# Zero-padded low key parts in the differential attention, and one buffer pool for raw and split weights

## The chip, the core and the metric

The kernel runs on one core of a Trainium2 chip. The metric is the device time of one execution in microseconds (us). Work goes to five engines that run at the same time: TensorE (PE in the profile; its weight loads are shown apart, as PEld), VectorE (DVE), ScalarE (ACT), GpSimd (POOL), and SyncE (SP), which here only issues DMAs.

## What is computed

One inference step of a two-layer diffusion backbone over 640 tokens: 512 latent tokens (a grid) and 128 context tokens. Each layer normalises its input, applies a shift and a scale, sends it through one input projection, runs three branches (latent attention "MLA", a short gated convolution, and differential attention), gates them, and adds the output projection to the residual. The change is in the differential attention, which has 4 heads with two score maps each:

```python
q = q.reshape(b, n, DIFF_HEADS, 2, DIFF_QK)          # DIFF_QK = 64
k_all = jnp.concatenate([k_ctx, rope(k)], axis=1)    # 512 latent + 128 cached keys
s = jnp.einsum('bqhad,bkhad->bhaqk', q, k_all) * scale
p = jax.nn.softmax(s, axis=-1)
a = p[:, :, 0] - lam_full * p[:, :, 1]
o = jnp.einsum('bhqk,bkhe->bqhe', a, v_all)
```

## The kernel before

Channels lie on the 128 partitions and tokens on the free axis; the 640 tokens are worked in two halves of 320 (`HB`). To get float32 accuracy from single-pass products, operands are split into a high part (rounded to `float32r`) and a low part (the rest); `mm3` (L347 to L352) makes three products of each pair: high with high, high with low, low with high.

**Input projection.** The weights come in 15 units per layer of mostly 256 columns, plus 4 units of the output projection. `load_unit` (L301) loads a unit in two halves into raw tiles (L307, L308), rounds them to the high part on ACT (L312), and subtracts on DVE, or on POOL for a few units, for the low part (L314). The raw tiles have a pool of 3 buffers (tag `raw`), the high and low tiles one of 9 (tag `w`, `wtiles`, L286). `unit(n, k=1)` asks for unit n and starts the next. The scratch tile `tb` of `silu_bcast` (L138) is a raw tile too.

**Differential attention, one head.** `q_post` (L537) rotates the queries and writes `qs[:, a, :]` for each of the two maps a: on the 64 partitions of that map the high part of q, on the other 64 its low part (L543, L544). `k_post` (L548) rotates the keys to `kf`, writes `kh[:, a, :]` (the high part of the map's keys on both halves of the partitions, L562 and L564) and the low part `kl` for all 128 channels at once, in one DVE instruction of 128x640 (L559). The tile `kl` is taken from the pool `blk` of 39 general slots (`slot`, `NBLK`).

`diff_unit` (L587) does 128 queries: for each map a and each half j of the keys two products into the same PSUM region, with `qs` as the stationary operand (loaded as weights, on PEld) and the keys as the moving one:

```python
TE.matmul(ps[:, j, 0:HB], qs[:, a, qc], kh[:, a, js], start=True, stop=False)    # L603: 128 rows
TE.matmul(ps[:, j, 0:HB], qs[own, a, qc], kl[own, js], start=False, stop=True)   # L604: 64 rows
```

The first contracts over 128 rows (high and low q with high k), the second over the map's own 64 (high q with low k). There are 2 layers x 4 heads x 4 query tiles x 2 maps x 2 halves = 128 of each. Then DVE takes the row maximum (L613), scales it (L614), ACT takes the exponential (L620), DVE the reciprocal (L622), the factor (L623) and the combination of both maps (L625); a later stage transposes (L582) and multiplies with the values (L634).

**Order.** The queues are filled by a program that interleaves generators: `main` (projections), `bg` (work of other engines: `q_post`, `k_post`, weight loads), `side` (the modulation vectors of this and the next layer: DMAs at L147 and pairs of multiply-and-sum instructions on DVE, L152), and the attention units. Each attention unit moves the projections on by 5 steps of 6 products. The framework then puts each engine's instructions in a fixed order, gives tiles their slots and sets the waits; an allocation waits until a slot of its tag is released. Each engine runs its queue in order.

Of the kernel before, what the change touches and what calls it, by code (L numbers as in the profile page):

```python
# [15 lines left out]
ALU = mybir.AluOpType  # L16
# [12 lines left out]
# the parts of the two halves of the tokens: from, to, stream  # L29
# [9 lines left out]
# The input projection is read in units of 256 columns (dv0, dv1: 272, for the rotary keys are with  # L39
# them; cq1: 128), in the order of use.  # L40
# [20 lines left out]
def tile_kernel(ctx: ExitStack, tc: tile.TileContext, i: dict, o: dict):  # L61
# [11 lines left out]
    NBLK, NW, NRAW = 39, 9, 3  # L73
# [17 lines left out]
    # ---------------------------------------------------------------- constants  # L91
# [19 lines left out]
    # products of zeros warm the tensor engine up while the first loads are under way  # L111
# [7 lines left out]
    # silu of the two conditioning vectors, with channels on partitions  # L119
# [6 lines left out]
    # modulation: mod[l][part] is [P, KT, 2 streams]  # L126
    mod = [[cst.tile([P, KT, 2], F32, name="mod%d_%d" % (l, s)) for s in range(3)] for l in range(DEPTH)]

    # the rest on the vector engine: rows of the transposed weights times the broadcast silu,
    # one half of the channels after the other  # L130
# [3 lines left out]
    def silu_bcast(hf, name):  # L134
        for c in range(2):
            pin(nc.sync.dma_start(out=cb2[:, c, :],
                                  in_=i["cond2"][c:c + 1, hf * 512:(hf + 1) * 512].broadcast_to([P, 512])))
        tb = wp.tile([P, 2, 512], F32, tag="raw", name="tb" + name, bufs=NRAW)  # L138
        S.activation(tb, cb2, AF.Tanh, scale=0.5)
        V.tensor_scalar(out=tb, in0=tb, scalar1=0.5, scalar2=0.5, op0=ALU.mult, op1=ALU.add)  # L140
        V.tensor_tensor(out=cb2, in0=cb2, in1=tb, op=ALU.mult)
# [14 lines left out]
    def ada_fin(l, s, ks=slice(0, KT)):  # L156
        """adds the bias; the scale becomes norm_g * (1 + scale)"""
# [9 lines left out]
    # -lambda of each layer, and subln * (1 - lambda_init) / 2  # L167
# [19 lines left out]
    # ---------------------------------------------------------------- helpers  # L187
    def rsqrt(v, n, name):
        """1/sqrt of a small [p, n] tile of positive numbers: a bit-level start y, then a y' = a y (t^2 + b t / a + c / a),
        t = v y^2, which is right to 2e-5, and a Newton step from there"""  # L190
# [14 lines left out]
    def rstd_half(accs, n, name):  # L205
        """accs, each [P, 320]: squares, to be summed over all of them and over the partitions; gives 1/rms on all
        partitions in PSUM. Three overlapping tiles of 128 tokens cover the half."""
# [15 lines left out]
    class Norm:  # L223
        """collects the squares of one half of the tokens over the k tiles"""
# [32 lines left out]
    bg = []            # work of the other engines that goes along with that of the tensor engine  # L257
# [7 lines left out]
    def split(src, name):  # L265
        """the halves of the tokens of src, each as a high and a low part"""
# [19 lines left out]
    def wtiles(w, name, tag):  # L286
        """room for the high and the low part of half a unit"""
        if tag == "w":
            return [wp.tile([P, 4, w], F32R, tag="w", name="w%s%s" % (c, name), bufs=NW, padded_shape=[P, 4, 272])
                    for c in "hl"]  # L290
        f = kh_tile if tag == "kh" else lambda nm: qs_tile(nm, T)
        return [f("w%s%s" % (c, name)).rearrange("p a n -> p (a n)")[:, 0:4 * w].rearrange("p (k c) -> p k c", k=4)
                for c in "hl"]
# [7 lines left out]
    def load_unit(src, w, name, tags, eng, res):  # L301
        """src [2, P, 4 * w] in DRAM -> tiles of the high and the low parts"""
        raws = []
        for hf in range(2):
            if hf == 1 and len(loaded) == 1:
                yield
            raws.append(wp.tile([P, 4, w], F32, tag="raw", name="r%s%d" % (name, hf), bufs=NRAW, padded_shape=[P, 4, 272]))  # L307
            pin(nc.sync.dma_start(out=raws[hf], in_=src[hf]), len(loaded) < 3)  # L308
        yield
        for hf in range(2):  # L310
            hi, lo = wtiles(w, "%s%d" % (name, hf), tags[hf])
# [16 lines left out]
    def unit(n, k=1, only_load=False, halves=2):  # L328
        """weights of unit n; those of the next k are on their way"""
# [12 lines left out]
    def wtile(n, kt, cs):  # L342
        """high and low parts of the columns cs of k tile kt of unit n"""
# [3 lines left out]
    def mm3(ps, aa, bb, first=True, last=True):  # L347
        """ps (+)= aa.T @ bb for operands split into high and low parts"""
# [5 lines left out]
    late = []          # low parts that are still to be taken  # L354

    def scaled(l, j, kt, rb, xs):
        """x / rms * norm_g * (1 + scale) of half j"""
# [7 lines left out]
    def modulate(l, j, kt, rb, xs, hs, last=False, t=None):  # L365
        """h = x / rms * norm_g * (1 + scale) + shift of half j, k tile kt, as high and low parts; the low part of a
        k tile follows the product of the next one"""
# [28 lines left out]
    # ---------------------------------------------------------------- start  # L396
# [9 lines left out]
    # Shift and scale of the first layer, in blocks of 512 columns: 0 and 1 of the shift, 2 and 3 of the scale. The  # L406
    # tensor engine sums three of them over the k tiles, the vector engine one, for which the tensor engine adds up the
    # partitions.
# [10 lines left out]
    def load_start(*what):  # L419
        """the next k tile of a block, or "x" for the first half of the next tile of x"""  # L420
# [78 lines left out]
    for l in range(DEPTH):  # L499
# [3 lines left out]
        def proj(nm, b, j):  # L503
            """128 columns (block b of unit nm) of half j of the tokens, channels on partitions"""
# [17 lines left out]
        def rope(dst, src, cos, sin, mask, name, rs=slice(0, P), eng=V):  # L522
            """dst = rotated latents of src, on the partitions rs"""
# [12 lines left out]
        # ------------------------------------------------ differential attention, one head  # L536
# [11 lines left out]
        def k_post(h, k, res):  # L548
# [6 lines left out]
            kl = slot("kl" + tg, F32R)  # L555
# [748 lines left out]
```

## Time and profile before

| what | value |
|---|---|
| device time, 3 runs | 873.0, 874.47, 876.0 us (median 874.47) |
| span of the profiled execution, first to last instruction | 871.4 us |
| PE busy | 836.4 us (96%) |
| DVE busy | 629.3 us (72%) |
| ACT busy | 445.4 us (51%) |
| mean granted TensorE clock | 0.983 |

The profile comes from one execution, for which no device time apart from its span is listed; the span is 1.6 us under the shortest of the three runs and 3.1 us under the median. "Busy" of PE counts overlapping products once. In a timeline, the distance from one product's start to the next is what a product costs; its duration is longer, since products overlap. An "idle before" entry names what ended the idle time.

### The profile page before, as it was taken

The numbers are of one execution on the slowest core, as the hardware profiler recorded it, in microseconds if no ns is written. First come the engines' busy times: TensorE is split into PE (matmuls) and PEld (weight loads), VectorE is DVE, ScalarE is ACT, GpSimd is POOL, SyncE is SP. The second block draws the span as 40 slices with busy tenths as digits, with TensorE's granted clock in tenths as the row PEclk, the third lists the DMA queues.
The fourth block names the chain that finished last, engine by engine and source line by source line (L and its number), as shares of the span: only waits on it lengthen the run. The fifth ranks groups of instructions, "written<-read, shape, count | busy, mean of one in ns | idle before, by whom it ended". The sixth has DMA issues, their size and how long they took to land.

```text
span 871.4 us, 14318 instructions
## 1 busy us (share of the span) xinstructions
PE 836.4 (96%) x5390; PEld 755.1 (87%) x5390; DVE 629.3 (72%) x1481; ACT 445.4 (51%) x978; POOL 70.3 (8%) x45
## 2 busy tenths in 40 slices
PE   6999999999999998999999999999999999999995
PEld 1399788888989897999999988888898999999994
DVE  4887887798878778689577778777667656667535
ACT  2265445454647566565345444545464666767210
POOL 3300020030000202000220002003000020200000
PEclk9999999999999999899999999999999999999997
DMA  8916343031401332134831324302030011110503
GB/s 316 364 44 212 104 125 116 24 120 63 147 21 61 94 118 66 39 109 147 280 97 43 124 74 128 121 19 77 4 103 25 26 49 49 49 50 16 179 1 120
DMA packets 66164, 85.52 MB, mean 98 GB/s; under 512 B 4976, under 2 KB 47408, under 8 KB 66096
## 3 DMA queue, kind: packets, MB, share of 16 engines
q1 hardware_dynamic: 65520, 83.96, 30.1%
q8 instruction: 42, 0.69, 0.3%
q10 hardware_dynamic: 576, 0.66, 0.2%
q14 instruction: 26, 0.21, 0.1%
HBM read 78.14 MB, written 6.46 MB: 97 GB/s over the span
## 4 chain that ended last, share of the span: by engine, by line
PE 70%; DVE 12%; ACT 8%; DMA 6%; issue 3%; SPq 1%; DVEq 0%; ACTq 0%
PE S L604 4%; PE wo L351 4%; PE wo L352 4%; PE wo L350 4%; PE S L603 4%; PE O L634 3%; DVE jk L152 2%; PE p1qk L350 2%; PE p1qk L352 2%; PE p1qk L351 2%; PE Om L906 2%; DMA ada<-in_adaA 2%; PE p0c L352 2%; PE tpm L889 2%; PE p1c L350 2%
## 5 line engine op out<-in xcount | busy, mean ns | idle before, releaser
L152 DVE CUSTOM_DVE_ANT_0 jk<-at,cb 128x512 bf16<-128x512 f32 x128 | 92.2, 720 | 2.0 <-DMA at<-in_adaT 1.1
L620 ACT ACTIVATE E<-S,sm 128x640 f32<-128x640 f32 (+1 forms) x80 | 56.0, 708 | 70.3 <-DVE sm L614 51.4
L351 PE MATMUL wo<-mx,who 128*128 128x320 f32 x256 | 79.2, 310 | 0.1
L352 PE MATMUL wo<-mx,wlo 128*128 128x320 f32 x256 | 78.9, 309 | 0.0
L350 PE MATMUL wo<-mx,who 128*128 128x320 f32 x256 | 78.4, 310 | 0.0
L613 DVE TENSOR_REDUCE sm<-S 128x1 f32<-128x640 f32 (+1 forms) x80 | 56.4, 714 | 25.1 <-PE S L604 24.3
L603 PE MATMUL S<-kh,qs 128*128 128x320 f32 x128 | 49.4, 386 | 3.7 <-ACT E L620 3.7
L604 PE MATMUL S<-kl,qs 64*128 64x320 f32 x128 | 52.6, 411 | 0.0
L878 ACT ACTIVATE Em<-Sm,smm 128x640 f32<-128x640 f32 (+1 forms) x40 | 28.4, 709 | 43.9 <-DVE smm L876 41.7
L351 PEld LDWEIGHTS wo<-mx,who 128*128 128x128 f32 x256 | 48.1, 188 | 0.7 <-DVE mx L273 0.4
L352 PEld LDWEIGHTS wo<-mx,wlo 128*128 128x128 f32 x256 | 48.1, 188 | 0.0
L235 ACT ACTIVATE sqn<-xn 128x320 f32<-128x320 f32 x32 | 15.1, 471 | 64.4 <-DVE xn L1152 62.6
L350 PEld LDWEIGHTS wo<-mx,who 128*128 128x128 f32 x256 | 47.8, 188 | 0.0
L352 PE MATMUL v<-whi_dv,hl 128*128 128x272 f32 x160 | 46.2, 289 | 0.0
L350 PE MATMUL v<-whi_dv,hh 128*128 128x272 f32 x160 | 46.1, 288 | 0.0
L351 PE MATMUL v<-wli_dv,hh 128*128 128x272 f32 x160 | 46.0, 288 | 0.0
L634 PE MATMUL O<-v,atd 128*128 128x128 f32 x336 | 43.9, 274 | 0.0
L314 POOL TENSOR_TENSOR wli_c<-ri_c,whi_c 128x1024 fp32r<-128x1024 f32 x8 | 20.5, 2562 | 280.1 <-PE p1zm L351 97.8
L350 PE MATMUL p0c<-hh,whi_c 128*128 128x320 f32 x128 | 42.1, 329 | 0.0
L350 PE MATMUL p0qk<-hh,whi_qk 128*128 128x320 f32 x128 | 40.6, 328 | 1.4 <-ACT hh L378 1.4
L634 PEld LDWEIGHTS O<-v,atd 128*128 128x128 f32 x336 | 41.9, 191 | 0.0
L604 PEld LDWEIGHTS S<-kl,qs 64*128 64x128 f32 x128 | 23.5, 184 | 21.2 <-issue 20.4
(375 smaller groups left out, 2669.9 us busy)
## 6 DMA issues: line engine op xcount, KB each, us to landing
at<-in_adaT SPq DMA_DIRECT2D x64, 256.0 KB, 3.9
ada<-in_adaA SPq DMA_DIRECT2D x32, 256.0 KB, 5.0
ri_qk<-in_wi SPq DMA_DIRECT2D x16, 512.0 KB, 4.1
ri_c<-in_wi SPq DMA_DIRECT2D x16, 512.0 KB, 3.7
ro<-in_wo SPq DMA_DIRECT2D x16, 512.0 KB, 4.1
ri_dv<-in_wi SPq DMA_DIRECT2D x8, 544.0 KB, 4.0
ri_zd<-in_wi SPq DMA_DIRECT2D x8, 512.0 KB, 3.9
x<-in_xT SPq DMA_DIRECT2D x16, 160.0 KB, 4.8
```

The source lines that it names most:

```text
L152: V.tensor_tensor_reduce(out=junk, in0=raw, in1=cb2[:, c, :], scale=1.0, scalar=0.0, op0=ALU.mult, op1=ALU.add, accum_out=acc)
L314: eng.tensor_tensor(out=lo, in0=raws[hf], in1=hi.bitcast(F32), op=ALU.subtract)
L350: TE.matmul(ps, ah, bh, start=first, stop=False)
L351: TE.matmul(ps, ah, bl, start=False, stop=False)
L352: TE.matmul(ps, al, bh, start=False, stop=last)
L603: TE.matmul(ps[:, j, 0:HB], qs[:, a, qc], kh[:, a, js], start=True, stop=False)
L604: TE.matmul(ps[:, j, 0:HB], qs[own, a, qc], kl[own, js], start=False, stop=True)
L613: V.tensor_reduce(out=sm[:, a:a + 1], in_=Sv[a], axis=AX.XY if u < 4 else AX.X, op=ALU.max)
L620: S.activation(ev, Sv[a], AF.Exp, bias=sm[:, 2 + a:3 + a], scale=DIFF_SCALE, accum_out=so)
L634: TE.matmul(po[:, 0:128], at[:, c * 128:(c + 1) * 128], vv[:, h * 128:(h + 1) * 128], start=c == 0, stop=c == n - 1)
L878: S.activation(e if u < 4 else e[:, 0:128], Sv, AF.Exp, bias=sm[:, 1:2], scale=MLA_SCALE, accum_out=sm[:, 2:3])
L889: TE.transpose(tp[:, c * 128:(c + 1) * 128], toktile(e, c), ident)
```

## The change

The low key parts get two permanent tiles, `klz[0]` and `klz[1]` (128x2x640 each), used in turn by the heads. `klz[h % 2][:, a, :]` holds the low part of map a on that map's own 64 partitions and zeros on the other 64; the zeros are written once, by `clear_klz`, in layer 0. The subtraction that makes the low part is done per map, on 64 partitions. The second product then has the same 128-row stationary operand as the first; the zeros cancel the rows of low q. Memory for this comes from the general slots (39 to 37), which hold no `kl` any more, and from the weights: raw and split weight tiles, and `tb`, share one pool of 11 buffers in place of 3 + 9. The rest of the diff removes comments.

```diff
-    NBLK, NW, NRAW = 39, 9, 3
+    NBLK, NW = 37, 11
...
-        tb = wp.tile([P, 2, 512], F32, tag="raw", name="tb" + name, bufs=NRAW)
+        tb = wp.tile([P, 1024], F32, tag="w", name="tb" + name, bufs=NW, padded_shape=[P, 1088])
+        tb = tb.rearrange("p (c n) -> p c n", c=2)
...
+    klz = [cst.tile([P, 2, T], F32R, name="klz%d" % n) for n in range(2)]
+
+    def clear_klz():
+        z = slot("klz0")
+        V.memset(z, 0.0)
+        for t in klz:
+            for a in range(2):
+                oth = slice(64 - a * 64, 128 - a * 64)
+                V.tensor_copy(t[oth, a, :], z[oth])
...
-            raws.append(wp.tile([P, 4, w], F32, tag="raw", name="r%s%d" % (name, hf), bufs=NRAW, padded_shape=[P, 4, 272]))
+            raws.append(wtile_new(w, "r%s%d" % (name, hf), "w", F32))
...
-            hi, lo = wtiles(w, "%s%d" % (name, hf), tags[hf])
+            hi = wtile_new(w, "wh%s%d" % (name, hf), tags[hf], F32R)
+            lo = wtile_new(w, "wl%s%d" % (name, hf), tags[hf], F32R)
...
-            kl = slot("kl" + tg, F32R)
+            kl = klz[h % 2]
             hk = slot("hk" + tg, F32R)
             S.copy(hk, kf)
             yield
-            V.tensor_tensor(out=kl, in0=kf, in1=hk.bitcast(F32), op=ALU.subtract)
             for a in range(2):
                 own, oth = slice(a * 64, a * 64 + 64), slice(64 - a * 64, 128 - a * 64)
+                V.tensor_tensor(out=kl[own, a, :], in0=kf[own], in1=hk[own].bitcast(F32), op=ALU.subtract)
                 S.copy(kh[own, a, :], kf[own, :])
...
-                    own = slice(a * 64, a * 64 + 64)
...
                         TE.matmul(ps[:, j, 0:HB], qs[:, a, qc], kh[:, a, js], start=True, stop=False)
-                        TE.matmul(ps[:, j, 0:HB], qs[own, a, qc], kl[own, js], start=False, stop=True)
+                        TE.matmul(ps[:, j, 0:HB], qs[:, a, qc], kl[:, a, js], start=False, stop=True)
...
             if l == 0:
+                clear_klz()
                 prep_small()
```

`wtile_new(w, name, tag, dt)` gives one tile of the tag that `wtiles` gave two of. `clear_klz` is called after the first five token tiles of the values' first half, before the attention of head 0 begins.

## Rows read from the trace of the kernel before

**Rows 1.** The page, parts 1 and 2: busy time of an engine with its share of the span, and the granted TensorE clock in 40 slices of the span, in tenths (9 is 90% or more).

```profile
PE 836.4 (96%) x5390; PEld 755.1 (87%) x5390; DVE 629.3 (72%) x1481; ACT 445.4 (51%) x978; POOL 70.3 (8%) x45
...
PEclk9999999999999999899999999999999999999997
```

**Rows 2.** The page, part 4: the chain of work that ended last, by engine and by engine and line.

```profile
PE 70%; DVE 12%; ACT 8%; DMA 6%; issue 3%; SPq 1%; DVEq 0%; ACTq 0%
PE S L604 4%; PE wo L351 4%; PE wo L352 4%; PE wo L350 4%; PE S L603 4%; PE O L634 3%; DVE jk L152 2%; PE p1qk L350 2%; PE p1qk L352 2%; PE p1qk L351 2%; PE Om L906 2%; DMA ada<-in_adaA 2%; PE p0c L352 2%; PE tpm L889 2%; PE p1c L350 2%
```

**Rows 3.** Groups of TensorE instructions by line and shape: tile written and tiles read, shapes, count, busy us and mean ns of one, idle before. S is the score tile of the differential attention, Sm that of the MLA.

```profile
L604 PE MATMUL S<-kl,qs 64*128 64x320 f32 x128 | 52.6, 411 | 0.0
L603 PE MATMUL S<-kh,qs 128*128 128x320 f32 x128 | 49.4, 386 | 3.7 <-ACT E L620 3.7
...
L351 PE MATMUL Sm<-kml,qmh 96*128 96x320 f32 x64 | 20.1, 314 | 0.0
```

**Rows 4.** Timeline of TensorE products around the scores of one unit (both maps, eight products) in layer 0: start us, duration us, line, tiles, shapes. The two last lines are projection products.

```profile
213.05 0.31 PE L603 MATMUL S<-kh,qs 128*128 128x320 f32 x1
213.29 0.41 PE L604 MATMUL S<-kl,qs 64*128 64x320 f32 x1
213.62 0.41 PE L603 MATMUL S<-kh,qs 128*128 128x320 f32 x1
...
215.34 0.41 PE L604 MATMUL S<-kl,qs 64*128 64x320 f32 x1
215.67 0.41 PE L350 MATMUL p0qk<-hh,whi_qk 128*128 128x320 f32 x1
215.93 0.31 PE L351 MATMUL p0qk<-hl,whi_qk 128*128 128x320 f32 x1
```

**Rows 5.** Timeline of the weight loads (PEld): two of that unit, with the idle time before them, and one of an MLA unit.

```profile
213.62 0.19 PEld L603 LDWEIGHTS S<-kh,qs 128*128 128x128 f32 x1 [0.15 <-issue]
213.97 0.18 PEld L604 LDWEIGHTS S<-kl,qs 64*128 64x128 f32 x1 [0.16 <-issue]
...
315.45 0.19 PEld L350 LDWEIGHTS Sm<-kmh,qmh 96*128 96x128 f32 x1
```

**Rows 6.** Timeline of TensorE: a score product of 128 rows and the 128-row product after it; then the first and the last of 17 products in a row of 320 columns, five of them scores of the MLA with 96 rows, the others projection products with 128.

```profile
266.13 0.31 PE L603 MATMUL S<-kh,qs 128*128 128x320 f32 x1
266.28 0.31 PE L350 MATMUL qp<-cqh,wuqh 128*128 128x320 f32 x1
...
315.31 0.31 PE L351 MATMUL Sm<-kml,qmh 96*128 96x320 f32 x1
...
317.65 0.31 PE L352 MATMUL p0c<-hh,wli_c 128*128 128x320 f32 x1
```

**Rows 7.** Windows: the stretch from the first to the last latent score product of layer 0, and of layer 1. After the window: its length, busy us (and instructions) of PE, PEld, DVE, ACT, POOL, the granted clock, the DMA share and GB/s.

```profile
90.90:273.50 182.60, 178.99 (x1095) 155.46 (x1094) 150.80 (x360) 94.98 (x235) 12.41 (x7) 0.99 0.28 88
...
504.90:688.10 183.20, 179.87 (x1094) 156.65 (x1092) 133.94 (x303) 94.75 (x231) 11.74 (x7) 0.98 0.22 66
```

**Rows 8.** The longest waits of DVE in these two stretches (two of layer 0, then two of layer 1): who waited for whom, us in total, times, longest us.

```profile
DVE sm L613 <- PE S L604: 9.4, 12, 1.5
DVE sm L622 <- ACT E L620: 8.9, 15, 1.4
...
DVE sm L613 <- PE S L604: 14.9, 21, 1.5
DVE sm L622 <- ACT E L620: 13.0, 15, 1.8
```

**Rows 9.** The longest wait of PE within the attention, over the whole span.

```profile
PE S L603 <- ACT E L620: 3.7, 6, 1.2
```

**Rows 10.** DVE instructions of single lines: count, duration ns as minimum/median/maximum, first and last start us, shapes.

```profile
L559 DVE TENSOR_TENSOR kl<-kf,hk x8: 815/823/827, 78.5 to 639.8; 128x640 fp32r<-128x640 f32 x8
...
L544 DVE TENSOR_TENSOR qs<-raw0qk,qs x8: 684/686/2699, 75.1 to 217.6; 64x512 fp32r<-64x512 f32 x8
...
L533 DVE TENSOR_TENSOR kf<-kf,shk x8: 675/684/699, 71.8 to 638.2; 128x512 f32<-128x512 f32 x8
...
L113 DVE MEMSET zero<- x1: 272/272/272, 0.9 to 0.9; 128x256 f32 x1
...
L824 DVE COPY kc<-kr x2: 420/710/1000, 182.9 to 597.4; 32x512 f32<-32x512 f32 x2
```

**Rows 11.** Timeline around the place of `clear_klz`: an idle time of DVE, the first maximum over latent scores, and the second map's first product on PE.

```profile
74.42 0.69 DVE L140 TENSOR_SCALAR tb<-tb 128x1024 f32<-128x1024 f32 x1 [1.90 <-ACT tb L139]
...
92.70 0.82 DVE L613 TENSOR_REDUCE sm<-S 128x1 f32<-128x640 f32 x1
...
93.75 0.42 PE L603 MATMUL S<-kh,qs 128*128 128x320 f32 x1 [0.78 <-ACT E L620]
```

**Rows 12.** The way of a weight unit: its DMA (KB, us from issue to landing), the rounding of one half on ACT, the subtraction of one half on DVE; and the longest wait of an SP load for a general slot.

```profile
ri_qk<-in_wi SPq DMA_DIRECT2D x16, 512.0 KB, 4.1
...
L312 ACT CAST whi_qk<-ri_qk x16: 1039/1050/1067, 32.0 to 587.0; 128x1024 fp32r<-128x1024 f32 x16
...
L314 DVE TENSOR_TENSOR wli_qk<-ri_qk,whi_qk x10: 1210/1219/1456, 35.0 to 590.6; 128x1024 fp32r<-128x1024 f32 x10
...
SPq L147 <- ACT qm L851: 10.8, 1, 10.8
```

More of the change, by code (lines that the diff above doesn't have):

```diff
@@ L284, in kh_tile, with wtile_new @@
         return blk.tile([P, 2, T], F32R, tag="kh", name=name, bufs=2)
-    def wtiles(w, name, tag):
+    def wtile_new(w, name, tag, dt):
         if tag == "w":
[L289 to L293, printed above, removed]
+            return wp.tile([P, 4, w], dt, tag="w", name=name, bufs=NW, padded_shape=[P, 4, 272])
+        t = kh_tile(name) if tag == "kh" else qs_tile(name, T)
+        return t.rearrange("p a n -> p (a n)")[:, 0:4 * w].rearrange("p (k c) -> p k c", k=4)
+    klz = [cst.tile([P, 2, T], F32R, name="klz%d" % n) for n in range(2)]
[6 more added lines that the diff above has]
+                V.tensor_copy(t[oth, a, :], z[oth])
     def pin(ins, yes=True):
```

## The prediction, made before the changed kernel was run

> **What bounds the kernel now.** I read the page from the top. PE is busy for 96% of the span and DVE for 72% [rows 1], and 70% of the chain that ended last is PE [rows 2]. The reader should see there that the two score lines of the differential attention, L603 and L604, each have as large a share of that chain (4%) as one of the three lines of the output projection. They have only 128 products each, so each of them must be dear.
>
> The groups by shape say how dear: 411 ns for the 64-row product, 386 for its 128-row partner, against 314 for a score product of the MLA, also of 320 columns [rows 3]. Durations overlap, so I went to the timeline and took distances between starts. In the eight score products of one unit they are 0.24 us at first, then about 0.34 [rows 4]. The weight loads show why: each begins only after an idle time of 0.15 to 0.16 us of the loader [rows 5], although its operand has long been there. A load of 0.19 us that is not hidden behind the running product makes the difference. It is not the score work as such: a lone 128-row L603 with a 128-row product behind it costs 0.15 us, and a run of 96-row score products of the MLA and 128-row projection products, with loads that follow without a gap, has 16 distances in 2.34 us, 0.146 each [rows 5, 6]. What sets the 0.34 apart is that 128-row and 64-row operands alternate.
>
> Then I asked who else is near its limit there. The windows of the two attention stretches have PE at 179.0 of 182.6 us and 179.9 of 183.2, DVE at 150.8 (83%) and 133.9 (73%) [rows 7]. So PE bounds both now, but in layer 0 DVE has little room.
>
> **The change part by part.** *The products.* From 213.05 to 215.93 there are the eight products and one projection product that also pays for the switch, nine distances: 2.88 us [rows 4]. At 0.146 us each they would take 1.31. That is 1.57 us per unit, and 2 layers x 4 heads x 4 query tiles are 32 units: 50.2 us, or 25.1 per stretch. The number of products and of weight loads stays the same; a 128-row load takes 0.19 us as does a 64-row one [rows 5].
>
> The Trainium skill has a rule that speaks against this: the page "TensorE: Matmul & The Clock Gate", section "Part 3: Packing small matmuls", says that a weight load overlaps with a running product only when the two use different row groups of the array. By that rule padding to 128 rows, which uses all row groups, would leave every load exposed and gain nothing. The trace disagrees: the loads of the MLA scores use the same rows as the products before them and are hidden, at 0.146 us a product [rows 5, 6].
>
> *The low keys.* One 128x640 subtraction of 0.82 us per head [rows 10] becomes two on 64 partitions. A 64-partition subtraction of 512 columns takes 0.686 us where a 128-partition one takes 0.684 [rows 10], so each of the two costs 0.82 again: 0.82 more per head, 6.6 in all, 2.5 in each stretch (three of a layer's four heads fall into it). Nothing waits longer for them in program order, since the copies of kh that follow end later.
>
> *Layer 0's stretch.* With PE alone it would shrink to 182.6 - 25.1 = 157.5. DVE needs 150.8 + 2.5 = 153.3 of that. Its idle time is 31.8 now, of which 9.4 is waiting for L604 and goes away [rows 7, 8]. If all the other 22.4 stayed, the stretch would take 175.7 and gain only 6.9. The 8.9 of waiting for the exponentials [rows 8] I expect to stay, since ACT gets no faster and DVE's order has nothing to put there: 162.2. Of the other 13.5, scattered over many small waits that begin with results of PE, I let 3 stay: 165, a gain of 17.6, between 6.9 and 25.1.
>
> *Layer 1's stretch.* PE alone: 158.1. DVE: 133.9 + 2.5 + 13.0 (exponentials) = 149.4, below it; with all its idle time but the 14.9 for L604 it would be 170.8 [rows 7, 8]. So PE stays the bound, and I let its idle time grow from 3.3 to 7, because the chain of maximum, exponential and next product through the two score buffers (PE waits for it 3.7 us in six places today [rows 9]) gets less cover: 162, a gain of 21, between 12.4 and 25.1.
>
> *clear_klz.* A memset of 256 columns takes 0.27 us, so 640 take some 0.7; each of the four copies of 640 columns lies between 0.4 (the shortest DVE copy, of 512 columns) and 1.25 (the longest, scaled by columns) [rows 10]: 2.3 to 5.7 us of DVE. What can hide it is that the first latent scores come at 90.9 [rows 7], and that DVE has a gap of 1.9 us shortly before its place [rows 11]. What is queued behind it are the `side` sums and two weight subtractions, then the first maximum at 92.7, at which PE already waits 0.78 [rows 11]; without cover PE would lose up to 4 us. I take 1.5.
>
> *Pools.* Two general slots fewer, but two `kl` tiles fewer to hold where they count, so within the attention nothing changes. Elsewhere (MLA, output projection, layer border) loads of the side sums already wait for slots, 10.8 us at most [rows 12]; DVE takes their data later than that. I take 0.5 us, with 6 as the upper bound. For the weights 9 + 3 buffers become 11. Eight hold the unit in use and the next one; before, that left 1 and 3 raw, now 3 for both. From its DMA to the low part half a unit needs 4.1 + 1.05 + 1.22 = 6.4 us [rows 12], and PE has 96 products x 0.147 = 14 us of work per unit. I take 0, and the missing cover appears as a rival.
>
> *Sum.* 17.6 + 21 - 1.5 - 0.5 = 36.6 us less than the profile's span of 871.4, so 834.8. The median of the runs lies 3.1 us above that span; I carry this over: 838.
>
> **The rivals.** *All of it arrives.* DVE's small idle times close up and PE bounds both stretches: 50.2 less about 1 elsewhere, 825. For it: DVE has run at 83% with PE nearly full, and its order need not change. Against it: 153.3 of 157.5 us is 97%, and DVE runs in order between PE and ACT.
>
> *DVE becomes the bound in both layers.* All idle time that is not for L604 stays: 6.9 + 12.4 = 19.3, less 3 elsewhere: 858. Shorter stretches in which PE waits could also cost clock: the granted clock is 0.98 to 0.99 there now [rows 7].
>
> *No gain on PE.* What exposes the loads is not the alternation but something that stays, for example that two products in a row load the same queries; then the distances stay at 0.34, the added DVE work is covered by PE as today, and the time is 874.5. Against it: in the MLA's triples the first two products share their queries too, and the run with them has 0.146 throughout [rows 6]. The rule of the Trainium skill weighed above would give this case's time as well; the trace speaks against it with the same rows.
>
> *Slower.* One mechanism: in the shared pool a raw half gets a buffer that the products of the unit two before still read, so that its load starts late and the 6.4 us of its way [rows 12] are exposed. There are 38 units; it eats the 36.6 us when it exposes 1 us per unit on average, and at 2 us per unit the time is 874.5 - 36.6 + 76 = 914. Against it: the 14 us of products per unit cover the way twice over, and the number of buffers left for raw tiles is the same 3.
>
> **How the numbers follow.** I give the forecast 0.54, with its own range of 830 to 846 (the middle of both stretches' bounds); all of it arriving 0.19; DVE in both layers 0.18; no gain 0.04; slower 0.05. The range reaches from 823 to 858: below it lies a small part of the second case (0.05), above it part of the third and the last two (0.15). A measurement can tell about 0.3%, or 2.6 us, from no change here. Faster takes the first three cases, 0.91; same 0.04; slower 0.05.
>
> **What would show it.** In the profile after, L604 should have 128 rows, and L603 and L604 about 312 ns each, with distances of 0.15 us and no "issue" gaps in their loads; if not, the first step is wrong. The stretches should be about 165 and 162 us long; DVE should be above 90% busy in layer 0's and around 84% in layer 1's; its wait for L604 should drop well below today's, and PE's idle time in the attention should rise by some 10 us, mostly in layer 0. PE waiting for a weight subtraction (L314) or a raw DMA (L308 before) would show the shared pool at fault. The prediction is wrong if DVE's fixed order turns out to hide less or more than I assume, which is its weakest step.

## The result, and the profile after

The changed kernel takes 838.86 us (median of 832.23, 837.55, 840.16 and 841.44) against 874.34 in four runs of before: a ratio of 0.958, with a 95% interval of 0.954 to 0.962. Six more runs in a later comparison have a median of 835.21, ratio 0.954 (0.951 to 0.958). The forecast of 838 holds. (A ratio is estimated from the single runs of both kernels; it can differ by up to 0.002 from the quotient of the two medians.)

The page after, parts 1 and 4 (busy time of an engine, then the chain that ended last, by engine), for [rows 1] and [rows 2]:

```profile
PE 783.8 (94%) x5390; PEld 739.3 (89%) x5390; DVE 633.4 (76%) x1494; ACT 445.8 (54%) x978; POOL 70.0 (8%) x45
...
PE 60%; DVE 18%; ACT 9%; DMA 7%; issue 3%; POOL 1%; SPq 1%; POOLq 0%; DVEq 0%; ACTq 0%
```

PE has the same 5390 products and lost 52.6 us of busy time. In the chain, PE fell from 70% to 60% and DVE rose from 12% to 18%.

The diff moves the lines: L603 and L604 are L614 and L615 now, L613 is L624, L620 is L631, L622 is L633, L350 to L352 are L362 to L364. The groups of products by shape, for [rows 3]:

```profile
L614 PE MATMUL S<-kh,qs 128*128 128x320 f32 x128 | 40.7, 327 | 8.5 <-ACT E L631 8.4 <-ACT atd L596 0.2
L615 PE MATMUL S<-klz,qs 128*128 128x320 f32 x128 | 38.5, 310 | 0.0
```

The timeline of PE in a unit of layer 0 (start, duration), then of its weight loads, for [rows 4, 5]:

```profile
99.00 0.31 PE L614 MATMUL S<-kh,qs 128*128 128x320 f32 x1
99.15 0.30 PE L615 MATMUL S<-klz,qs 128*128 128x320 f32 x1
99.29 0.31 PE L614 MATMUL S<-kh,qs 128*128 128x320 f32 x1
...
100.16 0.31 PE L362 MATMUL p0qk<-hh,whi_qk 128*128 128x320 f32 x1
```

```profile
98.86 0.19 PEld L614 LDWEIGHTS S<-kh,qs 128*128 128x128 f32 x1
99.01 0.19 PEld L615 LDWEIGHTS S<-klz,qs 128*128 128x128 f32 x1
```

From 99.00 to 100.16 there are eight distances: 0.145 us each, where they were 0.34. The loads have no bracket with an idle time behind them any more.

The windows of the five stages (length; busy us and instructions of PE, PEld, DVE, ACT, POOL; granted clock; DMA share; GB/s), for [rows 7]: up to the first latent score product, layer 0's attention, the middle (rest of layer 0 and layer 1's projections), layer 1's attention, and the end:

```profile
0.00:91.80 91.80, 80.83 (x458) 56.16 (x459) 68.61 (x168) 38.28 (x77) 15.79 (x19) 1.00 0.66 227
91.80:254.50 162.70, 154.37 (x1096) 149.81 (x1095) 149.66 (x358) 94.57 (x232) 12.34 (x7) 1.00 0.31 100
254.50:483.00 228.50, 221.30 (x1554) 214.39 (x1554) 171.44 (x413) 125.59 (x254) 19.98 (x8) 1.00 0.34 108
483.00:643.20 160.20, 155.03 (x1095) 151.18 (x1095) 133.85 (x304) 94.92 (x230) 12.16 (x7) 0.99 0.24 76
643.20:830.20 187.00, 172.27 (x1195) 167.75 (x1194) 109.83 (x255) 92.45 (x187) 9.73 (x4) 0.97 0.19 63
```

Of before, these are the windows of layer 0's attention, the middle, layer 1's attention and the end, cut at the same products:

```profile
91.00:273.50 182.50, 178.88 (x1095) 155.36 (x1093) 150.70 (x360) 94.92 (x234) 12.41 (x7) 0.99 0.28 88
273.50:504.90 231.40, 224.28 (x1554) 218.79 (x1554) 171.91 (x409) 124.93 (x252) 20.18 (x8) 0.98 0.35 109
504.90:688.40 183.50, 180.17 (x1095) 156.78 (x1093) 134.20 (x303) 95.05 (x231) 11.74 (x7) 0.98 0.22 65
688.40:871.40 183.00, 172.34 (x1196) 168.06 (x1195) 106.57 (x252) 91.17 (x185) 10.07 (x4) 0.97 0.19 61
```

In layer 0's attention, PE lost 24.5 us of busy time and the stretch 19.8; in layer 1's, 25.1 and 23.3 (all differences of attention windows are from these windows of 182.5 and 183.5 us). The start got 0.8 us longer, the middle 2.9 shorter, the end 4.0 longer. The sum is -41.2, the difference of the two spans. PE in the end stage is as busy as before (172.3): its idle time there rose from 10.7 to 14.7 us.

The granted clock is part of these numbers. The profiled execution after had a mean of 0.992, before 0.983. A stretch's clock is a mean of pieces at either of the two levels, 1.2 and 2.4 GHz: in the middle of before it was 0.50 from 298.7 to 302.1 us and from 346.4 to 353.2, and 1.00 otherwise; in the middle of after it was 1.00 throughout. The middle's 2.9 us are PE's busy time for the same 1554 products at these clocks. The attention stretches are touched too (0.99 and 0.98 before, 1.00 and 0.99 after); the part on DVE below compares them at equal clock. A second profile of the changed kernel has a span of 831.7 us at 0.988, with stages of 91.4, 164.1, 229.0, 160.2 and 187.0.

The waits after (who waits for whom: us in all, times, longest), for [rows 8, 9]:

```profile
DVE sm L624 <- PE S L615: 2.4, 4, 1.2
DVE sm L633 <- ACT E L631: 19.2, 26, 2.0
PE S L614 <- ACT E L631: 8.4, 6, 3.1
PE tpd L594 <- ACT E L631: 4.7, 4, 2.1
```

DVE's 24.3 us of waiting for score products in the two stretches are almost gone (2.4). PE's waiting for the exponentials grew from 3.7 us to 8.4 before score products, and from 3.1 to 4.7 before transposes.

### The profile page after: what moved, and what is told of

The parts are those of the page before. It is cut to its first block, busy times and chain, and to the rows that moved or that the text cites. A ratio compares the mean times of both kernels' runs of the same rounds, so it can differ in the third digit from the quotient of the medians.

```text
span 830.2 us, 14320 instructions
## 1 busy us (share of the span) xinstructions
PE 783.8 (94%) x5390; PEld 739.3 (89%) x5390; DVE 633.4 (76%) x1494; ACT 445.8 (54%) x978; POOL 70.0 (8%) x45
## 4 chain that ended last, share of the span: by engine, by line
PE 60%; DVE 18%; ACT 9%; DMA 7%; issue 3%; POOL 1%; SPq 1%; POOLq 0%; DVEq 0%; ACTq 0%
PE wo L363 5%; PE wo L362 4%; PE wo L364 4%; DVE jk L153 4%; DVE sm L624 2%; ACT E L631 2%; PE O L645 2%; PE p1c L362 2%; PE p1c L364 2%; PE p1c L363 2%; PE tpm L900 2%; PE p1qk L363 2%; PE p1qk L362 2%; PE S L614 2%; PE p1qk L364 2%
## 5 line engine op out<-in xcount | busy, mean ns | idle before, releaser
L153 DVE CUSTOM_DVE_ANT_0 jk<-at,cb 128x512 bf16<-128x512 f32 x128 | 91.9, 718 | 4.9 <-DMA at<-in_adaT 4.2
L631 ACT ACTIVATE E<-S,sm 128x640 f32<-128x640 f32 (+1 forms) x80 | 56.0, 706 | 61.4 <-DVE sm L625 43.3
L364 PE MATMUL wo<-mx,wlo 128*128 128x320 f32 x256 | 79.0, 309 | 0.0
L362 PE MATMUL wo<-mx,who 128*128 128x320 f32 x256 | 78.5, 310 | 0.0
L624 DVE TENSOR_REDUCE sm<-S 128x1 f32<-128x640 f32 (+1 forms) x80 | 55.3, 711 | 3.4 <-PE S L615 2.4
L614 PE MATMUL S<-kh,qs 128*128 128x320 f32 x128 | 40.7, 327 | 8.5 <-ACT E L631 8.4
L364 PEld LDWEIGHTS wo<-mx,wlo 128*128 128x128 f32 x256 | 48.1, 188 | 0.0
L362 PEld LDWEIGHTS wo<-mx,who 128*128 128x128 f32 x256 | 47.8, 188 | 0.0
L362 PE MATMUL v<-whi_dv,hh 128*128 128x272 f32 x160 | 46.3, 289 | 0.0
L364 PE MATMUL v<-whi_dv,hl 128*128 128x272 f32 x160 | 46.0, 288 | 0.0
L1164 DVE SCALAR_TENSOR_TENSOR xn<-wo,mod,xn 128x320 f32<-128x320 f32 (+2 forms) x48 | 19.6, 435 | 31.2 <-PE wo L364 21.4
L363 PE MATMUL p0qk<-hl,whi_qk 128*128 128x320 f32 x128 | 40.2, 315 | 2.4 <-DVE hl L394 2.4
L326 POOL TENSOR_TENSOR wli_c<-ri_c,whi_c 128x1024 fp32r<-128x1024 f32 x8 | 19.8, 2475 | 264.7 <-PE p0zm L363 85.4
L362 PE MATMUL p1c<-hh,whi_c 128*128 128x320 f32 x128 | 41.6, 325 | 0.0
L362 PE MATMUL p0c<-hh,whi_c 128*128 128x320 f32 x128 | 41.2, 322 | 0.0
```

The lines of the kernel that those rows point to most:

```text
L153: V.tensor_tensor_reduce(out=junk, in0=raw, in1=cb2[:, c, :], scale=1.0, scalar=0.0, op0=ALU.mult, op1=ALU.add, accum_out=acc)
L326: eng.tensor_tensor(out=lo, in0=raws[hf], in1=hi.bitcast(F32), op=ALU.subtract)
L362: TE.matmul(ps, ah, bh, start=first, stop=False)
L363: TE.matmul(ps, ah, bl, start=False, stop=False)
L364: TE.matmul(ps, al, bh, start=False, stop=last)
L624: V.tensor_reduce(out=sm[:, a:a + 1], in_=Sv[a], axis=AX.XY if u < 4 else AX.X, op=ALU.max)
```

## The experiments

In the table the stages are us of the profiled execution, cut at the same products as above.

| kernel | time, ratio to before (95%) | start | layer 0 attention | middle | layer 1 attention | end | clock |
|---|---|---|---|---|---|---|---|
| before | 874.34 | 91.0 | 182.5 | 231.4 | 183.5 | 183.0 | 0.983 |
| after | 838.86, 0.958 (0.954 to 0.962) | 91.8 | 162.7 | 228.5 | 160.2 | 187.0 | 0.992 |
| pools alone | 878.56, 1.000 (0.997 to 1.003) | 92.0 | 180.7 | 233.3 | 181.4 | 190.2 | 0.984 |
| 37 slots alone (one run) | 878.49 | 91.0 | 181.5 | 237.4 | 183.6 | 183.1 | 0.981 |
| pool of 11 alone (one run) | 877.89 | 91.5 | 181.7 | 230.0 | 184.7 | 188.2 | 0.984 |
| grouped order | 850.14, 0.970 (0.966 to 0.975) | 91.2 | 173.4 | 230.8 | 169.7 | 183.0 | 0.982 |
| half padded (one run) | 856.75 | 91.9 | 174.7 | 231.0 | 168.4 | 189.0 | 0.978 |
| before, short sums | 859.0, 0.980 (0.975 to 0.984) | 90.9 | 179.1 | 225.4 | 178.4 | 183.4 | 0.992 |
| after, short sums | 829.65, 0.947 (0.941 to 0.952) | 91.9 | 159.1 | 230.9 | 157.6 | 188.8 | 0.984 |
| after, no low products | 827.69, 0.943 (0.940 to 0.946) | 91.7 | 162.9 | 228.8 | 151.7 | 190.1 | 0.983 |

The runs of before beside the experiments had medians of 875.9 to 877.5 us.

**What makes the score products dear?** In the kernel before, the order within a map is changed, so that the number of rows changes half as often. Products, operands and shapes are the same:

```diff
                     for j in range(2):
                         js = slice(j * HB, (j + 1) * HB)
                         TE.matmul(ps[:, j, 0:HB], qs[:, a, qc], kh[:, a, js], start=True, stop=False)
+                    for j in range(2):
+                        js = slice(j * HB, (j + 1) * HB)
                         TE.matmul(ps[:, j, 0:HB], qs[own, a, qc], kl[own, js], start=False, stop=True)
```

> The kernel before with one change: within a map the two 128-row products of the halves come first, then the two 64-row ones, so operands change their row count twice per map instead of four times. Theory (the change of the row count exposes a load): the second 128-row and the second 64-row product start 0.15 us after the one before; the excess per unit falls from 1.57 to about 0.8 us, TensorE saves 25 us and the time falls by 18 to 25 us, to about 853. Rival (a 64-row product is slow by itself): all 64-row products stay 0.34 us behind the one before, and the gain is at most 12 us. Rival by the rule that loads are hidden only between different row groups: the two 64-row products use the same rows, so no gain.

Half of PE's excess went: its busy time fell by 11.7 and 14.0 us in the two stretches. The time fell by 27 us between the medians, a little more than the 18 to 25 expected, and by 23.3 between the profiled spans. The timeline of PE and of the loads for one unit (two products or loads of a pair in one line, with their joint duration):

```profile
207.98 0.45 PE L603 MATMUL S<-kh,qs 128*128 128x320 f32 x2
208.36 0.56 PE L606 MATMUL S<-kl,qs 64*128 64x320 f32 x2
208.86 0.56 PE L603 MATMUL S<-kh,qs 128*128 128x320 f32 x2
209.34 0.56 PE L606 MATMUL S<-kl,qs 64*128 64x320 f32 x2
209.83 0.41 PE L350 MATMUL p0qk<-hh,whi_qk 128*128 128x320 f32 x1
```

```profile
207.84 0.33 PEld L603 LDWEIGHTS S<-kh,qs 128*128 128x128 f32 x2
208.36 0.29 PEld L606 LDWEIGHTS S<-kl,qs 64*128 64x128 f32 x2 [0.19 <-issue]
208.86 0.30 PEld L603 LDWEIGHTS S<-kh,qs 128*128 128x128 f32 x2 [0.20 <-issue]
209.34 0.29 PEld L606 LDWEIGHTS S<-kl,qs 64*128 64x128 f32 x2 [0.19 <-issue]
```

There is one bracket per pair, at each change of the number of rows, in both directions. Where one product of a pair after a change alone lasts 0.41 (the last line of PE), a pair lasts 0.56: the second product comes 0.15 us behind, a 64-row product too. So the price belongs to the change of row count, not to 64-row products as such, nor to two loads on the same rows.

**Half of the maps padded.** In the changed kernel, map 1's low products go back to 64 rows:

```diff
-                        TE.matmul(ps[:, j, 0:HB], qs[:, a, qc], kl[:, a, js], start=False, stop=True)
+                        rs = slice(0, P) if a == 0 else slice(64, P)
+                        TE.matmul(ps[:, j, 0:HB], qs[rs, a, qc], kl[rs, a, js], start=False, stop=True)
```

> The changed kernel, but the second product of map 1 contracts over the 64 rows 64 to 127 alone, as before; map 0 keeps the padded 128 rows. All VectorE work and all memory are those of the changed kernel. Theory (each change of the row count exposes a load): map 0's four products are 0.146 us apart, map 1's 0.34; the excess per unit is half of 1.57 us, the time half way between both kernels, 850 to 862 us. Rival (the gain has another source in the changed kernel): nearer to 838 or to 875.

The groups of the low products, which share a line here:

```profile
L616 PE MATMUL S<-klz,qs 64*128 64x320 f32 x64 | 26.7, 417 | 0.0
L616 PE MATMUL S<-klz,qs 128*128 128x320 f32 x64 | 19.6, 314 | 0.0
```

Within one execution, the padded half has the price of after and the other half that of before. The time of the single run lies half way, 856.75 between 876.9 (before, beside it) and 835.2 (after, beside it).

**The memory part alone.** The pools of the changed kernel (37 slots, 11 shared buffers), with the products and the `kl` slot of before:

```diff
-    NBLK, NW, NRAW = 39, 9, 3
+    NBLK, NW = 37, 11
...
```

> The memory part alone: 37 general slots, one pool of 11 weight buffers, low keys from a general slot in one 128x640 subtraction, second score product on 64 rows as before. Theory (the gain is the padding, the pools are neutral): within 0.3% of the kernel before, 872 to 877 us; score products still about 0.34 us apart. Rival (the pools bring part of the gain, as they also end waits of the loads for raw buffers): faster by 5 us or more. Second rival (the pools cost, and the padding hides it): slower by 3 us or more.

The total is unchanged: ratio 1.000. But the stages are not the old ones. The attention stretches are 1.8 and 2.1 us shorter, the end is 7.2 longer. In layer 0, 16 products moved from the stretch to the middle; in the end, 5.3 us are idle time of PE and 1.9 its busy time at a clock of 0.96 in place of 0.97. So its two parts were run apart:

> The kernel before with one number changed: 37 general slots in place of 39, weight pools 9 and 3 as before. It asks which half of the memory part brings the 4 us of extra TensorE idle time that the changed kernel and the memory part alone show after layer 1's last latent score product (14.7 and 16 us idle there against 10.7 before). Theory (fewer slots move instructions in the queues of the MLA stage): idle time after the last score product 14 us or more. Rival (the shared weight pool does it): 10.7 us as before. Stretches as before, 182.5 and 183.5.

> The other half alone: one pool of 11 weight buffers, 39 general slots, low keys and products as before. Theory (slots, not the weight pool): TensorE idle after layer 1's last latent score product 10.7 us as before. Rival (the weight pool): 14 us or more. Either way no wait of TensorE for a weight subtraction or a raw load above 1 us in all.

With 37 slots the end stays as it was (183.1; PE idle 10.7 us); 16 products move from layer 0's attention to the middle. With the pool of 11 the end takes 188.2, in this window:

```profile
687.90:876.10 188.20, 172.30 (x1195) 167.81 (x1195) 108.79 (x252) 91.41 (x185) 9.73 (x4) 0.98 0.19 62
```

PE's busy time there is that of before, its idle time 15.9, 5.2 us more. Three waits in this stage make up the difference; of the second, before has 0.2 us, of the others nothing:

```profile
PE vm L817 <- DVE vm L822: 2.1, 1, 2.1
PE Sm L361 <- ACT Em L889: 1.8, 3, 1.2
PE tpm L900 <- ACT Em L892: 1.6, 1, 1.6
```

After has the same three, of 2.1, 0.6 and 1.5 us, and 4.0 us more idle time than before. The first wait comes from one instruction of DVE that stands ahead of `vm` in its queue and takes 2.19 us in place of 0.17 (before, then the pool of 11):

```profile
703.59 0.17 DVE L196 TENSOR_TENSOR w_d<-y_d 128x5 f32<-128x5 f32 x1
703.05 2.19 DVE L197 TENSOR_TENSOR w_d<-y_d 128x5 f32<-128x5 f32 x1
```

All nine profiles with the shared pool have it at this place, the five others don't; what makes the instruction slow stays open. Behind the other two waits is a late weight load. The rounding of a weight half stands in ACT's queue ahead of the `Em` that PE waits for, and ACT itself waits for the raw half (before, then the pool of 11):

```profile
753.22 1.04 ACT L312 CAST who<-ro 128x1024 fp32r<-128x1024 f32 x1
762.49 1.04 ACT L323 CAST who<-ro 128x1024 fp32r<-128x1024 f32 x1 [2.41 <-DMA ro<-in_wo]
```

In before this load was issued at 731.77, 21.5 us ahead of the rounding; here at 758.29, 4.2 us ahead, after a wait for a subtraction on POOL (L325). The rounding at 736.91, ahead of the second wait, waits 3.8 us for its load. The expectation that the slots were at fault fell; that no wait for a raw load would reach PE held for PE's own waits, but not for those through ACT.

**Separate pools again.** In the changed kernel, pools of 9 and 2 in place of 11:

```diff
-    NBLK, NW = 37, 11
+    NBLK, NW, NRAW = 37, 9, 2
...
```

> The changed kernel with the 11 weight buffers kept apart again, 9 for split and 2 for raw weights (and the scratch tile of the modulation), 37 general slots. Theory (the shared pool puts the rounding of weights later in ScalarE's order and so costs some 4 us of TensorE idle time after layer 1's last score product): that idle time falls from 14.7 back to about 11 us and the whole time to 830 to 835, ratio to the kernel before 0.948 to 0.954. Rival (two raw buffers make the loads late instead): slower than the changed kernel, TensorE waits for weight subtractions or their raw loads.

The end's idle time falls from 14.7 to 12.8 us, half of what had come; about 11 was expected. The slow instruction and the wait before transposes are gone. But with two raw buffers ACT waits 3.3 us for the same load, and PE 1.9 us for an `Em` behind it: the rival of this expectation, in part. The time is 839.07, ratio 0.957 (0.953 to 0.960), where 830 to 835 was expected: nothing won. Its profiled execution is the longest of six (846.23, clock 0.972; layer 0's attention 172.6 us at 0.95), so the other stages say little.

**Is DVE the limit?** The sums of the modulation vectors are cut to 64 of their 512 columns, in before and in after:

```diff
-V.tensor_tensor_reduce(out=junk, in0=raw, in1=cb2[:, c, :], scale=1.0,
+V.tensor_tensor_reduce(out=junk[:, 0:64], in0=raw[:, 0:64], in1=cb2[:, c, 0:64], scale=1.0,
...
```

> The kernel before, but the multiply-and-sum instructions of the modulation (L152) take 64 of their 512 columns, so that the modulation is a part of the sum only; some 55 us of VectorE work are gone, everything else stays. Theory (TensorE bounds both attention stretches before): the stretches stay within 3.5 us of 182.6 and 183.2 (the idle time that TensorE has there), the whole time falls by at most 8 us. Rival (VectorE holds the kernel already): a fall of 15 us or more.

> The changed kernel with the same cut in the modulation sums. Theory (after the change VectorE, 92% busy in layer 0's stretch, takes part of the gain there): layer 0's stretch falls from 162.8 to about 158, the 157.5 that TensorE needs; layer 1's from 160.2 to about 159; the time falls by 4 us or more beyond what the same cut gives the kernel before, to about 828 to 833. Rival (the idle time left on TensorE is the latency of the chain maximum, exponential, next product, not VectorE's load): the stretches stay within 1.5 us and the fall is the same as for the kernel before.

Windows with short sums: layer 0's and layer 1's attention in before, then layer 0's in after:

```profile
90.90:270.00 179.10, 177.03 (x1094) 154.03 (x1093) 126.68 (x359) 96.20 (x235) 11.64 (x7) 1.00 0.29 89
495.40:673.80 178.40, 178.27 (x1094) 155.84 (x1094) 122.71 (x304) 95.60 (x231) 11.66 (x7) 0.99 0.22 67
```

```profile
91.90:251.00 159.10, 154.78 (x1095) 151.34 (x1095) 127.04 (x357) 95.37 (x234) 11.37 (x7) 0.99 0.32 102
```

DVE is relieved of 24.0 us (before) and 22.6 (after) in layer 0's attention. That stretch gets 3.4 us shorter in before and 3.6 in after; layer 1's gives 5.1 and 2.6. After the change that brings PE's idle time in layer 0 down from 8.3 to 4.3. The surprise was before: 18.5 us between the medians, where at most 8 were expected, and 14.2 between the profiled spans. Of the 14.2, PE's busy time for the same products is 6.4 (836.4 to 830.0), at a clock of 0.992 in place of 0.983; the other 7.8 are idle time of PE, 4.8 of them in the two stretches and 2.1 in the middle. So the kernel before was not purely bound by PE: DVE cost it some 8 us of idle time already. That the cut would give after more than before was expected and did not come: 18.5 us against 5.6 to 9.2. Why the clock was higher in before with short sums (0.991 or 0.992 in all its runs) and not in after (0.982 to 0.986) stays open.

These windows compare PE at equal clock. With short sums the products of before keep it busy for 177.0 us in layer 0's stretch at 1.00 and for 178.3 in layer 1's at 0.99; after has 154.4 and 155.0 at the same clocks. So the padding saves PE 22.7 and 23.2 us, and the 24.5 and 25.1 between the first two profiles hold some 2 us of clock each.

**Which engine sets the length now?** In the changed kernel the low products are left out:

```diff
-                        TE.matmul(ps[:, j, 0:HB], qs[:, a, qc], kh[:, a, js], start=True, stop=False)
-                        TE.matmul(ps[:, j, 0:HB], qs[:, a, qc], kl[:, a, js], start=False, stop=True)
+                        TE.matmul(ps[:, j, 0:HB], qs[:, a, qc], kh[:, a, js], start=True, stop=True)
```

> The changed kernel without the products of the low key parts (128 products fewer, the scores lack high q with low k); the subtractions that make them stay. TensorE needs 128 x 0.146 = 18.7 us less, 9.3 in each stretch. Theory (TensorE is still the bound of both stretches after the change, with 5 to 8 us of idle time): both stretches shrink by 6 to 9.3 us, 162.7 to 154 to 156 and 160.2 to 151 to 154, and the time falls by 12 to 18 us. Rival (VectorE is now the bound in layer 0: 149.7 us busy and 5.8 us of waits for the exponential): layer 0's stretch stays at 159 or more, and the time falls by 11 us at most.

Windows of the two stretches:

```profile
91.70:254.60 162.90, 149.96 (x1032) 143.31 (x1031) 148.20 (x358) 93.91 (x230) 13.68 (x7) 0.98 0.31 98
483.40:635.10 151.70, 144.49 (x1032) 139.95 (x1031) 132.02 (x304) 93.76 (x229) 13.41 (x7) 1.00 0.26 80
```

Each has 64 products fewer, 9.3 us at 0.146. Layer 1 gives 8.5 of them back. Layer 0 gives nothing against the first profile of after (162.7, at 1.00 in place of 0.98) and 1.2 us against the second (164.1, at 0.98 too): PE is idle for 13 us instead. The whole time falls by 7.5 to 11.2 us, as the rival of this expectation had it. So layer 1's attention is still bound by PE, while layer 0's is set by DVE (148.2 of 162.9 us busy) and the waits between the engines.

**Two attempts to go further.** The copy `hk` is dropped, and the low part taken from `kh`:

```diff
-            hk = slot("hk" + tg, F32R)
-            S.copy(hk, kf)
...
-                V.tensor_tensor(out=kl[own, a, :], in0=kf[own], in1=hk[own].bitcast(F32), op=ALU.subtract)
                 S.copy(kh[own, a, :], kf[own, :])
+                V.tensor_tensor(out=kl[own, a, :], in0=kf[own], in1=kh[own, a, :].bitcast(F32), op=ALU.subtract)
```

> The changed kernel without the tile hk: the low part is taken from the high part that kh already holds on a map's own partitions, so one ScalarE copy of 128x640 (0.73 us) per head and one general slot per head are gone; the low part comes after the first copy of kh. Theory (ScalarE has slack, and the slots cost a little): between no change and 4 us faster than the changed kernel, 835 to 840 us, ratio to the kernel before 0.952 to 0.958. Rival (the low part comes later and the first product of a head waits): slower by 2 us or more.

It takes 837.9 us, ratio 0.956 (0.952 to 0.959): no difference from after. The other attempt gives DVE fewer sums in layer 0's attention, every sixth step in place of every fourth, beside a repeat of the changed kernel:

```diff
-    SIDES = (8, 4, 5)
+    SIDES = (8, 6, 5)
```

> The changed kernel once more, on the chip of the two that follow, for a profile at another granted clock than the first one (0.992, where the kernel before had 0.983) and for a narrower interval. Theory (some 8 us of the 41 us between the two profiled spans is clock): at a mean clock of 0.983 to 0.985 its span is 836 to 840 us, the ratio to the kernel before 0.955 to 0.962, the stretches 162 to 166 and 160 to 163 us. Rival (the first profile is typical): span 830 to 833 at the same clock as the kernel before.

> The changed kernel with the modulation sums spread thinner over the attention: one step of them for 6 steps of the projections in place of 4 (SIDES 8, 4, 5 becomes 8, 6, 5); nothing is left out, the rest of the sums falls into the MLA stage and the output projection, where VectorE has 25% idle. Theory (VectorE is the bound of layer 0's stretch after the change): that stretch falls by 2 to 4 us towards the 157.5 that TensorE needs, the whole time by 1 to 4 us against the changed kernel. Rival (the sums come late, and the output projection or layer 1's start waits for them): no change or slower by up to 5 us.

The repeat gave the 835.21 told above; its profile, at 0.988, lies between the two cases of its expectation. With fewer sums DVE is busy for 139.2 us in layer 0's attention and the stretch takes 161.6. But the sums are then still missing when the middle needs them; its window, and PE's two longest waits in it:

```profile
254.00:498.50 244.50, 228.13 (x1555) 220.36 (x1554) 182.09 (x441) 124.86 (x254) 20.23 (x8) 0.97 0.34 108
```

```profile
PE st_n L212 <- DVE sqn L245: 5.8, 1, 5.8
PE wo L362 <- DVE mod L1033: 3.8, 1, 3.8
```

The middle takes 244.5 us in place of 229 (8.6 of it idle time of PE, 6.9 its busy time at a clock of 0.97 in place of 1.00), and the kernel 851.06, ratio 0.971. The load of DVE in layer 0's attention can be moved, but it is needed before the next layer.

## Why the prediction was right

*The products.* The mechanism is the one forecast, and the distance forecast as 0.146 is 0.145. The 25.1 us of PE per stretch came as 24.5 and 25.1 in the profiles, but at equal clock they are 22.7 and 23.2: the term was some 2 us too large per stretch, and the clock hid it. The grouped order shows the cause, which the prediction had inferred from the rows of before. The rival that two loads of the same queries expose each other fell: they follow each other in the changed kernel, hidden.

*The low keys and the zeros.* The added DVE work is as worked out. Subtractions of the low keys, copies and memset, by line:

```profile
L573 DVE TENSOR_TENSOR klz<-kf,hk 64x640 fp32r<-64x640 f32 x16 | 13.1, 819 | 2.8 <-ACT hk L569 2.5
...
L304 DVE CAST klz<-klz 64x640 fp32r<-64x640 f32 x4 | 2.0, 488 | 0.1
...
L300 DVE MEMSET klz<- 128x640 f32 x1 | 0.6, 592 | 0.2 <-issue 0.2
```

13.1 less the 6.6 of before is 6.5, where 6.6 were expected; the zeros cost 2.6 us of DVE, near the lower bound of 2.3. The start grew by 0.8 and 0.4 us in the two profiles, not by 1.5.

*Layer 0's attention.* 162.7 and 164.1 us in the two profiles, forecast 165. The forecast let 11.9 us of DVE's idle time stay; 13.0 stayed. It put the waits for the exponentials at 8.9, and they are 5.8 in this stretch, the remainder being small waits. DVE's busy time did not grow to 153.3: it is 149.7, with 358 instructions where 363 would be the old ones and three more, so some of the background work fell outside the shorter stretch. So DVE was busy for less than forecast and idle for longer, and the errors partly cancel.

*Layer 1's attention.* 160.2 us in both profiles, forecast 162. PE's idle time is 5.2, where 7 were allowed. PE as the bound is what leaving out the low products showed. The 10 us of added idle time, "mostly in layer 0", are some 6.5 in the first profile (4.7 and 1.8).

*The pools.* This is the step that was wrong. The weight pool was costed at nothing, since a unit's products cover the way of the next weights and as many buffers are left for raw tiles. But the end stage is 4.0 us longer in both profiles, and the run with the pool alone shows that the pool is what does it. Some 2 us are the one slow DVE instruction, whose reason is open. The remainder is the rival of exposed loads in a small form: in after, the raw half is issued 4.1 us ahead of its rounding, ACT waits 2.3 us for it, and PE 1.5 us for what stands behind it in ACT's queue. The prediction looked for PE waiting for a subtraction or a raw load, and that did not come. In the pool-alone run part of it came back in the attention (layer 0's stretch 0.8 us shorter, PE idle 2.1 in place of 3.6).

*The sum.* 36.6 us were forecast and 41.2 measured between the profiled spans. The gain is 2.2 and 2.3 us larger in the two stretches and 0.7 at the start; middle and end together cost 1.1 where 0.5 was allowed. Part of the excess is clock: at 0.982 and 0.983 the changed kernel took 837.3 to 841.4 us, at 0.987 and 0.988 833.9 to 835.5. The difference of the medians, 35.5 and 41.7 us in the two comparisons, encloses the forecast of 36.6. That 838 lies within 1 us of 838.86 is luck: the gain was 4.6 us larger than forecast between the profiled spans, but the profiled execution was the shortest of the four, and the median lies 8.7 us above its span, not the 3.1 carried over from before.

## What to carry to other kernels

Read what a product costs from the distance between starts, and look at the brackets (idle times) of the weight loads beside it: an idle time at every other load points to something in the sequence, and a changed order of the same products tells what. Zero rows in an operand cost nothing on TensorE here (0.145 us from start to start; 0.146 between products without padding), and where padding is too dear, grouping the products by row count gives a part of it (27 of the 35 to 42 us). After PE's work is cut, ask stage by stage who is next, and don't take a shared pool for neutral because TensorE's work covers the loads: a load that starts later can hold up another engine's queue, and TensorE behind it. Compare stages at equal clock before a term counts as confirmed.

## What the runs showed of the hardware

When 128-row and 64-row products alternate, they start 0.34 us apart, and 0.145 us apart when all have 128 rows. The difference is about as long as a weight load (0.18 to 0.19 us), which begins only after an idle time of the loader at each change, in both directions; 96-row and 128-row products follow each other at 0.146 us without it [rows 6]. The Trainium skill, page "TensorEngine Tiling (Array Packing)", section "Tiling Modes", has a line that fits: "Changing tiling mode (not just tile) drains the TensorE". It gives no price; the runs here do. What the array does meanwhile is not in the traces, only that the load begins late.

The same kernel on one core gets different mean clocks in different executions, and its time moves with it: before took 871.7 us at 0.985 and 880.8 at 0.973. Differences of less than about 5 us between single executions of this kernel say little before the clock is compared. Within an execution the clock is 0.50 in short pieces, six in before's profile (the last at its end) and two in after's, but three in after's second profile.

One DVE instruction on 128x5 elements took 2.19 us in place of 0.17, at the same place in all nine profiles with the shared pool and in none of the others. The traces don't say why.
